# A decoder trunk's causal mask: from a product on TensorE to VectorE's reduction, with the forget gates' sums as rows of a score product

## The chip, the cores and the metric

The kernel runs on one core of a Trainium2 chip. The metric is the device time of one execution in microseconds (us), as the median of several runs. The engines are TensorE (PE: matmuls; PEld: its weight loads), VectorE (DVE), ScalarE (ACT), GpSimd (POOL) and SyncE (SP), whose queue issues nearly all transfers. Each engine works through its own queue in order and waits on semaphores of the others.

## What is computed

A trunk of two layers over 1024 tokens of width 1024. Layer 0 mixes tokens by differential attention (8 heads, each with two score maps), layer 1 by forgetting attention (16 heads, with a gate whose logarithm is summed along the tokens). After each comes a gated MLP with a short convolution. Cut to what matters here:

```python
# layer 0, per block of 128 queries
s = jnp.einsum('bhcqd,bhckd->bhcqk', qb, k) * scale
p = masked_softmax(s, causal_mask(start, Q_BLOCK, S))
a = p[:, :, 0] - lam * p[:, :, 1]
# layer 1
c = jnp.cumsum(jax.nn.log_sigmoid(f_logit + b_f), axis=1)
s = (jnp.einsum('bhqd,bhkd->bhqk', qb, k) * scale
     + cb[..., :, None] - c[..., None, :])
p = masked_softmax(s, causal_mask(start, Q_BLOCK, S))
```

## The kernel before

All big products run as several products of rounded fp32 (fp32r) halves: a value is split into a high part, made by ScalarE (L87), and the rest, made by VectorE (L89), and a product of two split values is three matmuls (`mm3`, L98 to L100). For the scores the halves are stacked: a head has 64 rows, so one matmul over 128 rows holds high times high and low times high (L496), and a second one holds high times low (L497), with a zeroed copy `qz` of the queries that GpSimd fills (L489).

The attention of a layer runs over 8 pairs of heads. For each pair there are 16 score jobs (8 query tiles of 128 for each of two heads or maps). A job of query tile qt covers (qt + 1) x 128 keys in chunks of 512. Between the jobs `attention` steps through the projection of the next pair (48 steps of three 512-wide matmuls), or, for the last pair, through the first half of the output projection (64 steps). These matmuls fill TensorE while VectorE and ScalarE do the softmax; `tick` and `tock` run the later parts of earlier jobs (normalisation, transposes by L1320, value products by L1345 and L98 on `pt`). So the order of the code sets the work, and a scheduler then sets each engine's order.

In a job TensorE first makes the scores in one of two PSUM banks `s`, and then adds the causal mask onto the last 128 columns by one more product: the identity in bf16 (`idb`) as weights and the mask (`mneg` in layer 0, `mpos` in layer 1, whose scores are negated) as the moving operand (L498). In layer 0 VectorE then takes the negated maximum (L517) and ScalarE the exponential with its sum (L520). In layer 1 VectorE adds, in one instruction with the minimum, the gates' sum of each key (L642). For that the sums, which are along one row, are broadcast to all partitions by a transfer (`load_ck`, L621, into the pool `lg`); `cq` holds the queries' sums (L645).

The sums are made at the start of layer 1: `forget_gates` makes the running sums within blocks of 128, and `forget_sums` adds the sums of the blocks ahead by a product with `tri` (L610), stores them to DRAM (L613) and transposes them for `cq` (L615). `first_pair` projects the first pair of heads, with nothing else to fill TensorE. In layer 0 the normalisation after the values uses a product with ones (L549) over squares made by ScalarE (L545).

Of the kernel before, what the change touches and what calls it, by code (L numbers as in the profile page):

```python
# [9 lines left out]
F32 = mybir.dt.float32  # L10
# [44 lines left out]
class Trunk:  # L55
# [64 lines left out]
    def consts(self):  # L120
# [147 lines left out]
    def split_q(self, par, src, scale, sl, lo):  # L268
# [6 lines left out]
    def split_k(self, par, src, sl):  # L275

        a, b = par[0][:, sl], par[1][:, sl]
        self.split(a, par[2][:, sl], src)
        self.move((b[64:], a[64:]), (b[:64], a[64:]), (a[64:], a[:64]))

# [42 lines left out]
    def first_pair_rotary(self, t):  # L323
# [10 lines left out]
        for c in range(2):  # L334
# [7 lines left out]
            for s in range(2):  # L342
                self.result(0, s, c, ps[s], dst[s], t)
# [4 lines left out]
        for c in range(2):  # L348
# [3 lines left out]
            self.result(0, 2, c, ps, dst[2], t)  # L352
# [4 lines left out]
            self.after(2 + 2 * c, self.turn_v, 0, c, dst[2], *t[5:], True)  # L357
        self.ahead(4)

    def first_pair(self, l, t):  # L360
# [4 lines left out]
        for c in range(2):  # L365
            if c == 1:
                self.transposes(self.acc, 1, range(2))
                self.turn_v(l, 0, dst, *t[5:])
# [3 lines left out]
            for s in range(3):  # L372
# [4 lines left out]
                self.result(l, s, c, ps, dst if s == 2 else None, t)  # L377
            if c:
                self.forget_sums()
                self.after(3, self.turn_v, l, c, dst, *t[5:], True)  # L380

    def project(self, l, p, t):
# [5 lines left out]
        for n, (s, c) in enumerate(order):  # L388
# [15 lines left out]
            self.after(D_EV, self.result, l, s, c, ps, dst[s], t)  # L404
# [5 lines left out]
            if s == 2:  # L410
                self.after(D_V[c], self.turn_v, l, c, dst[2], *t[5:], True)
# [3 lines left out]
    def result(self, l, s, c, ps, dst, t):  # L415

        sl = slice(c * 512, c * 512 + 512)
        if dst is not None:
            self.nc.scalar.activation(dst[:, sl], ps, AF.Copy, scale=DH ** -0.5 if s == 0 else 1.0)
        elif s == 0:  # L420
            if c == 0:
                self.qlo = self.tp.tile([P, 1024], F32R, tag="t", name=self.nm("ql"))
            self.split_q(t[:2], ps, -DH ** -0.5, sl, self.qlo[:, sl])
        else:
            self.split_k(t[2:5], ps, sl)

    def halves(self, dst, t, c, j):

        sl = slice(c * 512, c * 512 + 512)
        if j == 0:  # L430
            self.split_q(t[:2], dst[0][:, sl], None, sl, dst[0][:, sl].bitcast(F32R))
        else:
            self.split_k(t[2:5], dst[1][:, sl], sl)
# [1099 lines left out]
```

## Time and profile before

| | us |
|---|---|
| median of 3 runs | 2475.31 (2471.26 to 2476.17) |
| the profiled execution | 2474.66 |
| its span, first to last instruction | 2472.8 |
| attention of layer 0, about | 45 to 530 |
| MLP of layer 0, about | 530 to 1200 |
| attention of layer 1, about | 1214 to 1770 |
| MLP of layer 1, about | 1770 to 2472 |

The mean granted clock of TensorE is 0.998 of full. Durations of matmuls overlap: a matmul's row gives its start and the time until its modelled end, and the next may start long before it. What a matmul costs in a stream is therefore read from start to start. An arrow at a row's end names what ended the idle time ahead of the instruction. The page's other engines are averages over the span; whether they matter is read from who waits for whom.

### The profile page before, as it was taken

What the parts mean: (1) busy time and instruction counts of PE and PEld (TensorE: products, weight loads), DVE (VectorE), ACT (ScalarE), POOL (GpSimd) and SP (SyncE); (2) the same over time, 40 slices, a digit from 0 to 9 for tenths busy, and PEclk for the clock granted to TensorE, in tenths of its full rate; (3) what the DMA queues carried; (4) which work ended last, traced back from release to release, by engine and by line L of the source; (5) the groups of instructions that cost most, each with busy time, mean ns of one, the idle gap of its engine ahead of it and who ended that gap; (6) DMA issues with size and microseconds to landing.
All of it is one profiled execution on the core that took longest, in us unless ns stands there. A gap on an engine that the chain in (4) does not pass through costs nothing. (4 is left out here: it accounts for less than half of the span.)

```text
span 2472.8 us, 33965 instructions
## 1 busy us (share of the span) xinstructions
PE 2436.3 (99%) x12059; PEld 2016.7 (82%) x12059; DVE 1908.3 (77%) x3604; ACT 1256.4 (51%) x2387; POOL 136.3 (6%) x316
## 2 busy tenths in 40 slices
PE   8999999999999999999999999999999999999998
PEld 6888888788888888888778888888888888888886
DVE  5777777989866677887767777778898666668977
ACT  4555655646544444544545555555465444445444
POOL 2001000110000000000101000000010000000000
PEclk9999999999999999999999999999999999999999
DMA  5222222622222223974322222225222222238851
GB/s 174 71 86 79 76 81 84 216 72 99 77 102 78 77 77 131 343 238 154 107 87 78 78 77 76 78 85 172 86 86 102 86 77 77 92 99 315 273 170 68
DMA packets 116793, 289.50 MB, mean 117 GB/s; under 512 B 18032, under 2 KB 25072, under 8 KB 116624
## 3 DMA queue, kind: packets, MB, share of 16 engines
q1 hardware_dynamic: 115824, 285.44, 34.8%
q8 instruction: 95, 1.56, 0.3%
q0 software_dynamic: 800, 1.90, 0.2%
q14 instruction: 74, 0.61, 0.1%
HBM read 196.70 MB, written 59.11 MB: 103 GB/s over the span
## 5 line engine op out<-in xcount | busy, mean ns | idle before, releaser
L98 PE MATMUL m<-xh,wh 128*128 128x512 f32 x768 | 323.1, 421 | 11.2 <-ACT xh L87 10.9
L100 PE MATMUL m<-xh,wl 128*128 128x512 f32 x768 | 303.7, 395 | 0.0
L99 PE MATMUL m<-xl,wh 128*128 128x512 f32 x768 | 301.1, 392 | 0.0
L98 PE MATMUL m<-xh,wo 128*128 128x512 f32 x656 | 255.5, 389 | 0.5 <-ACT pt L1042 0.5
L100 PE MATMUL m<-xh,wo 128*128 128x512 f32 x656 | 255.5, 389 | 0.0
L99 PE MATMUL m<-xl,wo 128*128 128x512 f32 x656 | 255.2, 389 | 0.0
L87 ACT ACTIVATE wo<-wg 128x512 fp32r<-128x512 f32 x168 | 106.2, 632 | 222.4 <-PE m L100 215.8
L87 ACT ACTIVATE pt<-m 128x512 fp32r<-128x512 f32 (+1 forms) x240 | 128.5, 553 | 151.3 <-PE m L1320 112.7
L98 PE MATMUL m<-q,wo 128*128 128x512 f32 x472 | 184.3, 390 | 0.0
L99 PE MATMUL m<-q,wo 128*128 128x512 f32 x472 | 183.8, 389 | 0.0
L100 PE MATMUL m<-q,wo 128*128 128x512 f32 x472 | 183.7, 389 | 0.0
L98 PEld LDWEIGHTS m<-xh,wh 128*128 128x128 f32 x768 | 145.8, 190 | 34.4 <-ACT xh L87 10.9
L100 PEld LDWEIGHTS m<-xh,wl 128*128 128x128 f32 x768 | 144.8, 189 | 32.2 <-DVE wl L89 0.4
L89 DVE TENSOR_TENSOR pt<-m,pt 128x512 fp32r<-128x512 f32 (+1 forms) x240 | 148.5, 633 | 22.2 <-ACT pt L87 19.6
L99 PEld LDWEIGHTS m<-xl,wh 128*128 128x128 f32 x768 | 145.9, 190 | 23.1
L87 ACT ACTIVATE wo<-t 128x512 fp32r<-128x512 f32 x132 | 82.7, 627 | 145.3 <-PE m L100 133.3
L89 DVE TENSOR_TENSOR wo<-wg,wo 128x512 fp32r<-128x512 f32 x168 | 115.4, 688 | 38.5 <-ACT wo L87 37.7
L98 PEld LDWEIGHTS m<-xh,wo 128*128 128x128 f32 x656 | 123.1, 188 | 26.7 <-ACT pt L1042 1.3
L100 PEld LDWEIGHTS m<-xh,wo 128*128 128x128 f32 x656 | 123.1, 188 | 26.3 <-DVE wo L89 0.8
L99 PEld LDWEIGHTS m<-xl,wo 128*128 128x128 f32 x656 | 123.1, 188 | 25.6
L489 POOL CAST qz<-q 64x128 fp32r<-64x128 f32 x256 | 94.4, 370 | 888.4 <-PE s L498 793.2
L496 PE MATMUL s<-q,q 128*128 128x512 f32 (+3 forms) x384 | 130.3, 339 | 0.8 <-ACT p L650 0.8
(333 smaller groups left out, 6165.4 us busy)
## 6 DMA issues: line engine op xcount, KB each, us to landing
wst<-in_w SPq DMA_DIRECT2D x46, 512.0 KB, 3.4
t<-in_wi SPq DMA_DIRECT2D x44, 512.0 KB, 4.3
ha<-ad SPq DMA_DIRECT2D x88, 256.0 KB, 6.2
wg<-in_wi SPq DMA_DIRECT2D x42, 512.0 KB, 3.2
ad<-t SPq DMA_DIRECT2D x42, 512.0 KB, 3.5
q<-q SPq DMA_DIRECT2D x128, 128.0 KB, 2.3
pt<-in_wd SPq DMA_DIRECT2D x24, 512.0 KB, 5.3
hb<-in_wd SPq DMA_DIRECT2D x44, 256.0 KB, 4.5
```

Source lines behind the costliest of these rows:

```text
L87: nc.scalar.activation(hi, src, AF.Copy, scale=1.0 if scale is None else scale)
L89: nc.vector.tensor_tensor(lo, src, hi.bitcast(F32), op=ALU.subtract)
L98: mm(out, wh, xh, start=start, stop=False)
L99: mm(out, wh, xl, start=False, stop=False)
L100: mm(out, wl, xh, start=False, stop=stop)
L489: nc.gpsimd.tensor_copy(qz[r:r + 64, :], q[r:r + 64, qt * P:qt * P + P])
L496: nc.tensor.matmul(sb[:, ks], q[:, qt * P:qt * P + P], kd[:, ks], start=True, stop=False)
```

## The change

The mask's product goes, with its weights and the bf16 identity. A row `mask` of 1024 columns is made instead: zeros, and the negated mask in the last 128 columns. VectorE adds its last (qt + 1) x 128 columns to the scores in the instruction that takes their minimum, in both layers; the scores of layer 0 are negated now as well (by the scale on the queries), and their exponential has a scale of -1. In layer 1 the sums of the keys are no longer broadcast. They are split into a high and a low part, stored to DRAM, and read back as rows 64 and 65 beside the 64 low rows of the keys, which for the second head lie in a tile of their own (`kb`, filled by a transfer). The second score product runs over these 66 rows, with ones in rows 64 and 65 of `qz`, so that both heads use rows 0 to 65. The gates' weights `wf` lie in a working buffer of the pool `prob` in place of one of their own.

```diff
-        self.idb = cp.tile([P, P], BF16, name="idb")
-        nc.vector.tensor_copy(self.idb, self.ident)
-        self.mneg = cp.tile([P, P], BF16, name="mneg")
-        nc.vector.tensor_copy(self.mneg, mask)
-        self.mpos = cp.tile([P, P], BF16, name="mpos")
-        nc.vector.tensor_scalar(self.mpos, mask, -1.0, None, op0=ALU.mult)
+        self.mask = cp.tile([P, S], BF16, name="mask")
+        nc.gpsimd.memset(self.mask[:, :S - P], 0.0)
+        nc.vector.tensor_scalar(self.mask[:, S - P:], mask, -1.0, None, op0=ALU.mult)
...
-        self.move((b[64:], a[64:]), (b[:64], lo[64:]), (a[64:], lo[:64]))
...
+        hi = slice(0, 64) if l else slice(64, P)
+        lo_ = slice(64, P) if l else slice(0, 64)
+        self.move((b[hi], a[64:]), (b[lo_], lo[64:]), (a[64:], lo[:64]))
...
+    def split_k(self, l, p, t, src, sl):
...
+        a, b, lo = t[2][:, sl], t[3][:, sl], t[4][:, sl]
+        self.split(a, lo, src)
         self.move((b[64:], a[64:]), (b[:64], a[64:]), (a[64:], a[:64]))
+        if l:
+            self.move((t[7][:64, sl], lo[64:]))
+            if p:
+                self.sum_rows(p, t, sl)
+
+    def sum_rows(self, p, t, sl):
...
+        for h in range(2):
+            self.nc.sync.dma_start(t[4 + 3 * h][64:66, sl].bitcast(F32), self.cd[:, 2 * p + h, sl])
...
-    def scores(self, q, kd, kl, r, qt, mask):
+    def scores(self, l, q, kd, kl, h, qt):
...
+        r, rows = (0, slice(0, 66)) if l else (64 * h, slice(0, P))
...
             nc.tensor.matmul(sb[:, ks], q[:, qt * P:qt * P + P], kd[:, ks], start=True, stop=False)
-            nc.tensor.matmul(sb[:, ks], qz, kl[:, ks], start=False, stop=not last)
-        nc.tensor.matmul(sb[:, ln - P:ln], self.idb, mask, start=False, stop=True)
-        return sb, ln
+            nc.tensor.matmul(sb[:, ks], qz[rows], kl[rows, ks], start=False, stop=True)
+        mn = self.small(tag="nm")
+        nc.vector.tensor_tensor_reduce(sb[:, :ln], sb[:, :ln], self.mask[:, S - ln:], 1.0, BIG,
+                                       ALU.add, ALU.min, mn)
+        return sb, ln, mn
...
-        nc.vector.tensor_reduce(nmx, sb[:, :ln], axis=AX.X, op=ALU.max, negate=True)
...
-        nc.scalar.activation(pt[:, :ln], sb[:, :ln], AF.Exp, bias=nmx, accum_out=lsum)
+        nc.scalar.activation(pt[:, :ln], sb[:, :ln], AF.Exp, bias=mn, scale=-1.0, accum_out=lsum)
...
-            self.wf = [self.cp.tile([P, 128], F32R, name=f"wf{j}") for j in range(2)]
+            w = self.tmp(F32R, pool=self.pp, tag="p")
+            self.wf = w[:, :P], w[:, P:2 * P]
+            for t in self.qz[0] + self.qz[1]:
+                nc.gpsimd.memset(t[64:66, :].bitcast(F32), 1.0)
...
-        nc.sync.dma_start(self.cd.rearrange("h (b t) -> (h b) t", t=P), c)
+        hl = self.chl[:, :P], self.chl[:, P:]
+        self.split(*hl, c)
+        self.cd = self.dr.tile([2, 16, 1024], F32, name="cd")
+        for j in range(2):
+            nc.sync.dma_start(self.cd[j].rearrange("h (b t) -> (h b) t", t=P), hl[j].bitcast(F32))
+        self.sum_rows(0, t, slice(0, 1024))
...
-        if qt == 0 and (p, h) not in self.ck:
-            self.load_ck(p, h)
-        ck = self.ck[p, h]
-        sb, ln = self.scores(t[h], t[2 + h], t[4], 64 * h, qt, self.mpos)
-        nc.vector.tensor_tensor_reduce(sb[:, :ln], sb[:, :ln], ck[:, :ln], 1.0, BIG,
-                                       ALU.add, ALU.min, mn)
+        sb, ln, mn = self.scores(1, t[h], t[2 + h], t[4 + 3 * h], h, qt)
```

TensorE's queue in layer 0, at a score job in the middle of a pair (L498 is the mask; L549 the product with ones of the normalisation; `pt` are transposed probabilities), before:

```order
L496 MATMUL s_1553<-q_567,q_565 128x512
L549 MATMUL m_1397<-sq_1412,ones 128x256
L497 MATMUL s_1553<-q_568,qz_303 128x512
L496 MATMUL s_1553<-q_567,q_565 128x256
L497 MATMUL s_1553<-q_568,qz_303 128x256
L498 LDWEIGHTS idb
L498 MATMUL s_1553<-mneg,idb 128x128
L98 MATMUL m_1562<-pt_1512,q_569 128x256
```

and of the change:

```order
L507 MATMUL s_1523<-q_565,qz_300 128x512
L560 MATMUL m_1370<-sq_1385,ones 128x256
L506 MATMUL s_1523<-q_564,q_562 128x256
L507 MATMUL s_1523<-q_565,qz_300 128x256
L98 MATMUL m_1531<-pt_1482,q_566 128x256
```

The two entries of the mask are gone, and the product with ones stands behind the first two score products instead of between them; this second move is there in six of the pairs.

VectorE's queue in layer 0 around the reductions over the scores, before (L523 inverts a sum of exponentials, L89 is a split):

```order
L517 TENSOR_REDUCE nm_1948<-s_1944 128x1
L558 SCALAR_TENSOR_TENSOR of_1404<-sq_1873,of_1404 128x256
L89 TENSOR_TENSOR wl_2112<-wst_2009,wh_2111 128x1024
L517 TENSOR_REDUCE nm_1983<-s_1979 128x1
L89 TENSOR_TENSOR pt_1992<-m_1965,pt_1992 128x384
```

and of the change, in the same stage:

```order
L509 ISA s_1842,nm_1845<-s_1842,mask 128x256
L509 ISA nm_1845 128x1
L89 TENSOR_TENSOR pt_1883<-m_1856,pt_1883 128x512
L509 ISA s_1870,nm_1873<-s_1870,mask 128x256
L509 ISA nm_1873 128x1
L534 RECIPROCAL rs_1920<-ls_1847 128x1
```

One instruction becomes two: the addition with its minimum, and the read of the accumulator; what stands behind the read doesn't use its result.

TensorE's queue at the first scores of layer 1, from the product with `tri` on (L496 and L497 of the first query tile), before:

```order
L610 MATMUL m_11942<-p_11830,tri 128x1
L496 MATMUL s_11997<-q_11611,q_11609 128x128
L497 MATMUL s_11997<-q_11613,qz_300 128x128
L615 MATMUL m_11947<-ident,p_11830 128x128
L98 MATMUL m_11960<-xh_11391,wh_11912 128x512
```

of the change, the same place:

```order
L626 MATMUL m_11817<-p_11704,tri 128x1
L506 MATMUL s_11876<-q_11483,q_11481 128x128
L506 MATMUL s_11898<-q_11483,q_11481 128x256
L635 MATMUL m_11827<-ident,p_11704 128x128
L98 MATMUL m_11841<-xh_11260,wh_11787 128x512
```

and where the second products of these two tiles now stand, 37 products of 512 columns further on:

```order
L98 MATMUL m_11887<-xh_11646,wh_11787 128x512
L507 MATMUL s_11876<-q_11485,qz_297 128x128
L507 MATMUL s_11898<-q_11485,qz_298 128x256
L99 MATMUL m_11887<-xl_11647,wh_11787 128x512
L100 MATMUL m_11887<-xh_11646,wl_11788 128x512
```

The first products of two tiles stand together, and their second products, which need the sums' rows, have moved behind the filling work.

## Rows read from the trace of the kernel before

**Rows 1.** The page's part 1: engine, busy us (share), instructions.
```profile
PE 2436.3 (99%) x12059; PEld 2016.7 (82%) x12059; DVE 1908.3 (77%) x3604; ACT 1256.4 (51%) x2387; POOL 136.3 (6%) x316
```

**Rows 2.** Instructions of L498: engine, operation, count, duration ns min/median/max, first and last start.
```profile
L498 PE MATMUL s<-mneg,idb x128: 229/229/233, 49.2 to 514.7; 128*128 128x128 bf16 x128
L498 PE MATMUL s<-mpos,idb x128: 229/230/330, 1268.7 to 1766.5; 128*128 128x128 bf16 x128
```

**Rows 3.** TensorE's timeline, layer 0: start us, duration, engine, line, out<-in, shape.
```profile
307.15 0.23 PE L498 MATMUL s<-mneg,idb 128*128 128x128 bf16 x1
307.19 0.36 PE L98 MATMUL m<-pt,q 128*128 128x256 f32 x1
307.39 0.28 PE L99 MATMUL m<-pt,q 128*128 128x256 f32 x1
307.51 0.28 PE L100 MATMUL m<-pt,q 128*128 128x256 f32 x1
```

**Rows 4.** TensorE's timeline, layer 1, with and without a mask.
```profile
1405.21 0.38 PE L1320 MATMUL m<-ident,t 128*128 128x128 f32 x2
...
1405.66 0.40 PE L99 MATMUL m<-xl,wh 128*128 128x512 f32 x1
...
1407.95 0.22 PE L496 MATMUL s<-q,q 128*128 128x128 f32 x1
...
1408.12 0.23 PE L498 MATMUL s<-mpos,idb 128*128 128x128 bf16 x1
1408.16 0.48 PE L98 MATMUL m<-xh,wh 128*128 128x512 f32 x1
1408.48 0.39 PE L99 MATMUL m<-xl,wh 128*128 128x512 f32 x1
1408.71 0.40 PE L100 MATMUL m<-xh,wl 128*128 128x512 f32 x1
```

**Rows 5.** VectorE's groups by shape: line, operation, out<-in, count, busy us, mean ns.
```profile
L642 DVE CUSTOM_DVE_ANT_0 s<-s,ck 128x1024 f32<-128x1024 f32 x16 | 19.7, 1230 | 6.9 <-PE s L498 6.9
L517 DVE TENSOR_REDUCE nm<-s 128x1 f32<-128x1024 f32 x16 | 19.5, 1218 | 0.4 <-PE s L498 0.4
L642 DVE DVE_READ_ACCUMULATOR2_ANT nm<- 128x1 f32 x128 | 18.1, 141 | 0.0
```

**Rows 6.** VectorE's timeline around a reduction (layer 0) and the two-operand one (layer 1).
```profile
379.02 1.22 DVE L517 TENSOR_REDUCE nm<-s 128x1 f32<-128x1024 f32 x1
380.16 0.41 DVE L453 TENSOR_TENSOR t<-t,rope 128x256 f32<-128x256 f32 x1
1273.16 0.30 DVE L642 CUSTOM_DVE_ANT_0 s<-s,ck 128x128 f32<-128x128 f32 x1
1273.38 0.14 DVE L642 DVE_READ_ACCUMULATOR2_ANT nm<- 128x1 f32 x1
1273.38 0.35 DVE L654 TENSOR_SCALAR p<-p,rs 128x256 f32<-128x256 f32 x1
```

**Rows 7.** Timeline rows at waits, with idle time and its releaser in brackets.
```profile
306.14 0.70 PE L549 MATMUL m<-sq,ones 128*128 128x256 f32 x2 [0.33 <-ACT sq L545]
387.52 0.66 PE L465 MATMUL m<-ident,t 128*128 128x128 f32 x4 [0.98 <-DVE pt L89]
459.92 0.50 PE L98 MATMUL m<-wh,xh 128*128 128x512 f32 x1 [1.80 <-DVE pt L89]
1262.54 0.33 SPq L613 DMA_DIRECT2D cd<-p  x1
1264.82 1.53 SPq L621 DMA_DIRECT2D ck<-cd  x2
1270.67 0.30 DVE L642 CUSTOM_DVE_ANT_0 s<-s,ck 128x128 f32<-128x128 f32 x1 [3.49 <-DMA ck<-cd]
1272.24 0.33 PE L496 MATMUL s<-q,q 128*128 128x128 f32 x1 [0.81 <-ACT p L650]
```

**Rows 8.** Busy us (instructions) of PE, PEld, DVE, ACT, POOL in the fullest stretch; clock, DMA.
```profile
500.00:505.00 5.00, 5.00 (x27) 4.10 (x26) 5.00 (x9) 1.23 (x4) 0.00 (x0) 1.00 0.00 0
```

More of the change, by code (lines that the diff above doesn't have):

```diff
@@ L356, in first_pair_rotary @@
                 self.halves(dst, t, 1, 1)
-            self.after(2 + 2 * c, self.turn_v, 0, c, dst[2], *t[5:], True)
+            self.after(2 + 2 * c, self.turn_v, 0, c, dst[2], *t[5:7], True)
         self.ahead(4)
@@ L376, in first_pair @@
                 self.dense(ps, *self.w[s], c)
-                self.result(l, s, c, ps, dst if s == 2 else None, t)
+                self.result(l, 0, s, c, ps, dst if s == 2 else None, t)
             if c:
-                self.forget_sums()
-                self.after(3, self.turn_v, l, c, dst, *t[5:], True)
+                self.forget_sums(t)
+                self.after(3, self.turn_v, l, c, dst, *t[5:7], True)
     def project(self, l, p, t):
@@ L403, in project @@
                 dst[s] = self.tmp()
-            self.after(D_EV, self.result, l, s, c, ps, dst[s], t)
+            self.after(D_EV, self.result, l, p, s, c, ps, dst[s], t)
             if l == 0 and s == 1:
@@ L410, in project, with result @@
             if s == 2:
-                self.after(D_V[c], self.turn_v, l, c, dst[2], *t[5:], True)
+                self.after(D_V[c], self.turn_v, l, c, dst[2], *t[5:7], True)
             if c:
                 del self.w[i + s]
-    def result(self, l, s, c, ps, dst, t):
+    def result(self, l, p, s, c, ps, dst, t):
         sl = slice(c * 512, c * 512 + 512)
         if dst is not None:
-            self.nc.scalar.activation(dst[:, sl], ps, AF.Copy, scale=DH ** -0.5 if s == 0 else 1.0)
+            self.nc.scalar.activation(dst[:, sl], ps, AF.Copy, scale=-DH ** -0.5 if s == 0 else 1.0)
         elif s == 0:
@@ L514, in diff_scores @@
         nc = self.nc
-        sb, ln = self.scores(t[j], t[2 + j], t[4], 64 * j, qt, self.mneg)
-        nmx, lsum = self.small(tag="nm"), self.small(tag="ls")
-        nc.vector.tensor_reduce(nmx, sb[:, :ln], axis=AX.X, op=ALU.max, negate=True)
+        sb, ln, mn = self.scores(0, t[j], t[2 + j], t[4], j, qt)
+        lsum = self.small(tag="ls")
         yield
         pt = self.tmp(pool=self.wp, tag="wst", bufs=2) if j else self.tmp(pool=self.pp, tag="p")
-        nc.scalar.activation(pt[:, :ln], sb[:, :ln], AF.Exp, bias=nmx, accum_out=lsum)
+        nc.scalar.activation(pt[:, :ln], sb[:, :ln], AF.Exp, bias=mn, scale=-1.0, accum_out=lsum)
         yield
@@ L604, in forget_gates, with forget_sums @@
         self.c = c
-    def forget_sums(self):
+    def forget_sums(self, t):
         nc, c = self.nc, self.c
@@ L635, in fox_scores @@
         cq = self.cq[:, 2 * p + h, qt:qt + 1]
[L636 to L643 removed]
+        sb, ln, mn = self.scores(1, t[h], t[2 + h], t[4 + 3 * h], h, qt)
+        lsum = self.small(tag="ls")
         nc.vector.scalar_tensor_tensor(mn, mn, cq, cq, op0=ALU.subtract, op1=ALU.add)
[L646 to L647 removed]
         yield
@@ L670, in attention @@
         self.od = self.dr.tile([NP, P, 1024], F32, name=f"od{l}")
-        tiles = lambda p: [self.qtile((p + l) % 2) for _ in range(7)]
+        tiles = lambda p: [self.qtile((p + l) % 2) for _ in range(7)] + \
+            ([self.lp.tile([P, 1024], F32R, tag="lg", name=self.nm("kb"))] if l else [])
         self.slabs = [self.i[f"w{l}"][s * NP + p] for p in range(NP) for s in range(3)]
@@ L674, in attention @@
         self.w, self.stage, self.queue = {}, {}, []
-        self.ofs, self.ck = {}, {}
+        self.ofs = {}
         if l == 1:
```

33 lines of the change are left out of this document (10 added, 23 removed).

## The prediction

> **What bounds the kernel now.** I read the page's busy times first [rows 1]. TensorE is busy for 2436.3 of 2472.8 us, so only 36.5 us of the span can be anything but its own work; VectorE is busy for 77%. A saving on TensorE's path is therefore worth its full time as long as nothing else becomes late, and a cost on another engine is worth nothing as long as TensorE doesn't wait for it. Next I asked for the line that the change takes out: L498 has 128 matmuls in each layer, each with a weight load of the identity ahead [rows 2]. Then I read TensorE's timeline around a few of them, start to start, because the durations in the page overlap (a 512-wide matmul "takes" 0.39 us while the next starts 0.23 us later) and so say nothing about what one costs. Last come TensorE's waits, and the stretch where VectorE is fullest [rows 7, 8].
>
> **The change, part by part.**
>
> *The mask's product goes.* Behind a 256-wide score product the mask starts at 307.15, the next product (256 wide) at 307.19 and the one after that at 307.39 [rows 3]. Mask and one 256-wide product together take 0.24 us; the next product alone takes 0.12 us (307.39 to 307.51). The mask's price is 0.12 us: 0.04 of its own and 0.08 that shows as a longer step of the product behind it. Where the last score products are only 128 wide, the price is less: L496, L497, mask and one 512-wide product take from 1407.95 to 1408.48, 0.53 us, and two 128-wide transposes with a 512-wide product behind them, without a mask, from 1405.21 to 1405.66, 0.45 us [rows 4]. So 0.08 us there. With 512 columns behind it the mask costs 1408.16 to 1408.48 less the ordinary step 1408.48 to 1408.71, plus its own 0.04: 0.13 us. Two of the eight query tiles (tiles 0 and 4, whose last chunk is 128 wide) take the low price: 64 x 0.08 + 192 x 0.12 = 28.2 us. The bounds are 256 x 0.04 = 10.2 us, if the long step behind stays whatever stands in front of it, and 256 x 0.13 = 33.3 us. I take 28.2, since the two transposes show that a short product costs its 0.11 us each and leaves nothing behind ((0.45 - 0.23) / 2).
>
> The Trainium skill (TensorE: Matmul & The Clock Gate, Back-to-back issue gap) gives a 128-wide matmul at 2.4 GHz about 56 ns in a stream; by that alone the sum would be 14 us instead of 28. The rows disagree with it here: the step from mask to the second product behind is 0.12 us longer, not 0.06.
>
> *VectorE adds the mask, layer 0.* 128 maximum reductions become 128 of the two-operand instruction that layer 1 already uses, each with an accumulator read behind it. By durations this looks dear: 1230 for 1218 ns at 1024 wide, plus 141 ns for the read [rows 5], 0.153 us x 128 = 19.6 us. But the step decides. The two-operand one starts at 1273.16, its read at 1273.38, and the next, independent instruction starts at 1273.38 too [rows 6]: the read costs the engine nothing there. The step of 0.22 us is 0.08 below the duration of 0.30, just as the reduction's step of 1.14 us is 0.08 below its 1.22 (379.02 to 380.16) [rows 6]. What is left is the difference of durations, 0.012 us x 128 = 1.5 us over the 480 us of layer 0's attention, off TensorE's path. The exponential behind it waits for the read and starts some 0.14 us later; it frees a score bank that TensorE nowhere waits for in layer 0. I price this part at nothing, with 19.6 us as its upper end. In layer 1 the same instruction reads a bf16 mask in place of an fp32 row; no row of before shows that operand. Bounds: as now, or slower by the read of the other 128 (0.141 x 128 = 18 us, on an engine that idles for 23%); I take as now.
>
> *The gates' sums as two rows of the second product, layer 1.* The product keeps its columns and contracts 66 rows instead of 128. No matmul of before contracts fewer than 128 rows, so this isn't shown. The nearest rows are the 128-row products at 0.23 us for 512 columns [rows 4]; I take the same, and price the other end below as a rival. The Trainium skill (the same page, LDWEIGHTS) says that a weight load's time goes by its columns and that its row count doesn't matter, which speaks for no change. The sixteen broadcasts of a sum to all partitions (L621) go; per pair of heads and half there are three small transfers more, on SP's queue (one 64-row move, two of two rows). The transfer that overwrites two rows of what the move reads waits for it to land, 2.3 us by the gap between store and load in [rows 7], and behind it in SP's queue stand the next weight fetch and moves whose data are products steps away; price nothing, at worst 14 such waits of 2.3 us on a queue that no engine then waits for.
>
> *Layer 1's first scores.* Here the sums are now needed by TensorE itself, not only by VectorE. Now the sums are stored at 1262.54, their loads are issued at 1264.82, and VectorE, which waited 3.49 us for them, goes on at 1270.67 [rows 7]. After the change a split stands ahead of the store (two small instructions, some 0.6 us by VectorE's 0.3 us each [rows 6]), the store takes the same 2.3 us, and the small load between 2.3 us and the old one's 5.9: the rows are there between 1268 and 1271. The order puts the second products behind 37 further 512-wide ones after the sums' product, 37 x 0.23 = 8.5 us, so from about 1262 they stand past 1270. I take 1 us of loss there, 0 to 3 us as bounds; there is a wait of 0.81 us at this place already, for a score bank (1272.24) [rows 7].
>
> *What is late next.* TensorE now waits once per pair in layer 0 for the square that the normalisation takes (0.33 us at 306.14, with half a microsecond lost in all, between two score products); the order puts that product one place later, which gives back about 0.23 us x 6 = 1.3 us. Against it, TensorE arrives earlier at the waits for VectorE's splits: 0.98 us at 387.52 at the end of a pair, 1.80 us at 459.92 where the output projection begins [rows 7]. These chains run over VectorE and a weight fetch and don't become faster. Over the two or three score groups since the last meeting I take 0.25 us for each of 7 pairs = 1.8 us, and 1.3 us for each of the two last pairs, where VectorE is full (5.00 of 5.00 us at 500) [rows 8]: 2.6 us.
>
> *Small parts.* The mask's memset on POOL stands among the first memsets, which POOL has done long before the first scores; the gates' weights move into a working buffer, which is split after the down projection has released it, while ScalarE idles. Nothing.
>
> **Sum.** -28.2 - 1.3 + 1.0 + 1.8 + 2.6 = -24.1 us. The profiled execution took 2474.7 us (span 2472.8); that gives 2450.6, and against the median, 0.65 us higher, 2451 us.
>
> **The rivals.**
> 1. *The step behind remains.* The 0.08 us behind a mask is the price of going from a score group to another kind of product, and the last score product inherits it. Then between the mask's own step, 0.04 us, and the low price of 0.08 us goes everywhere: 10.2 to 20.5 us, 15 in the middle. With the other terms unchanged, 2475.3 - 15 - 1.3 + 5.4 = 2464. For it: the last score product is then what a different product follows. Against it: the transposes in rows 4 leave no such step. The Trainium skill's 56 ns per mask (section above) would end here too.
> 2. *VectorE's reads count in full.* If the reads wait in layer 0, 19.6 us stand on a queue that is full at each pair's end and in the last pair, and TensorE waits for it: 2451 + 19.6 = 2471, within the measurement. Against it: the step in rows 6.
> 3. *Slower: 66 rows cost more.* Layer 1's second products have 16 heads x 36 x 128 = 73,728 columns, at 0.23 us per 512 some 33 us. If a product over a part of the rows ran at half speed, this adds 33 us: 2484, slower than before. It decides from a factor of 1.7 (24 / 33 + 1). Nothing in the profile speaks for it.
> 4. *The change doesn't do what it says:* the order shows the 512 TensorE entries gone, so I leave this at nothing.
>
> **How the numbers follow.** Forecast 0.70 (2443 to 2460), rival 1 0.11, rival 2 0.07, rival 3 0.06; 0.06 for what I don't see. A measurement of this kernel can tell about 0.2%, 5 us, from no change. Faster: 0.70 + 0.11 + 0.04 = 0.85; same 0.07 + 0.01 = 0.08; slower 0.06 + 0.01 = 0.07. The range reaches from 2442 (33.3 saved, with nothing lost but the first scores' 1 us and some of the waits) to 2466, so that rival 1 is in it and no more than 2 in 10 is out.
>
> **What would show it.** In the changed profile: no L498; the product behind a 256- or 512-wide score group steps 0.12 or 0.23 us like its neighbours (rival 1: 0.2 or 0.32). VectorE's instruction behind an accumulator read in layer 0 starts with it (rival 2: 0.14 later, and longer TensorE waits for the splits). The step of a 512-wide second product in layer 1 stays at 0.23 us (rival 3: more). The wait at 459.92 grows by about a microsecond. TensorE's busy time falls by some 25 to 28 us, and its unbusy 36.5 us grow by at most 6. I'm wrong if the waits on VectorE or on the sums' transfers grow by more than 10 us together.

## The result and the profile after

The changed kernel takes 2455.6 us (median of 4 runs, 2455.07 to 2458.51) against 2475.05 for the kernel before (four runs, one more than in the table above): a ratio of 0.9926, interval 0.9909 to 0.9944, so 14 to 23 us less. The profiled execution took 2455.07 us, its span is 2453.3. The prediction was 2451.0 with a range from 2442 to 2466.

The page's part 1 of the changed kernel, to be held against [rows 1]:

```profile
PE 2414.2 (98%) x11803; PEld 2014.8 (82%) x11803; DVE 1911.1 (78%) x3731; ACT 1256.6 (51%) x2388; POOL 137.6 (6%) x321
```

TensorE has 256 products less and is busy 22.1 us less; of 2453.3 us it is not busy in 39.1, before in 36.5. VectorE's busy time hardly moves.

Where the time went, from the first scores of each layer, the first and last score product of each pair, and the first transposes of the MLPs, in the two traces:

| stretch | before, us | after, us | saved | 16 masks a pair at 0.091 |
|---|---|---|---|---|
| to the first score | 48.88 | 47.91 | 1.0 | |
| layer 0, pair 0 | 50.19 | 50.92 | -0.7 | 1.5 |
| layer 0, pairs 1 to 6 | 349.02 | 342.68 | 6.3 | 8.7 |
| layer 0, last pair to the MLP's transposes | 107.81 | 108.16 | -0.4 | 1.5 |
| MLP 0 and first pair's projection | 706.15 | 705.67 | 0.5 | |
| layer 1, pair 0 | 56.82 | 55.35 | 1.5 | 1.5 |
| layer 1, pairs 1 to 6 | 376.32 | 368.45 | 7.9 | 8.7 |
| layer 1, last pair to the MLP's transposes | 112.27 | 108.09 | 4.2 | 1.5 |
| MLP 1 | 665.32 | 666.06 | -0.7 | |

The two layers lose the same 128 masks, yet layer 1 becomes 13.5 us shorter and layer 0 only 5.2.

TensorE's timeline of the changed kernel, at a score group in layer 0 whose last product is 128 columns wide, at one whose last is 256 wide, and at a second score product over 66 rows in layer 1 (start us, duration, engine, line, out<-in, shape, idle time and its releaser):

```profile
269.60 0.27 PE L507 MATMUL s<-q,qz 128*128 128x128 f32 x1
269.71 0.33 PE L98 MATMUL m<-pt,q 128*128 128x256 f32 x1
269.88 0.28 PE L99 MATMUL m<-pt,q 128*128 128x256 f32 x1
...
303.13 0.47 PE L506 MATMUL s<-q,q 128*128 128x256 f32 x1
303.44 0.28 PE L507 MATMUL s<-q,qz 128*128 128x256 f32 x1
303.56 0.28 PE L98 MATMUL m<-pt,q 128*128 128x256 f32 x1
303.67 0.28 PE L99 MATMUL m<-pt,q 128*128 128x256 f32 x1
...
1393.43 0.39 PE L506 MATMUL s<-q,q 128*128 128x512 f32 x1
1393.66 0.40 PE L507 MATMUL s<-kb,qz 66*128 66x512 f32 x1
1393.89 0.28 PE L1354 MATMUL m<-pt,q 128*128 128x256 f32 x1
```

Behind the 256-wide group the next product now steps 0.11 us (303.56 to 303.67) like its neighbours, where behind a mask it stepped 0.20 [rows 3]: no long step remains. Behind the 128-wide group a part of it remains without any mask: 0.17 us (269.71 to 269.88), and 0.171 in the median of 35 such places. The 66-row product steps 0.23 us (1393.66 to 1393.89), as 128 rows do.

VectorE's timeline around a 1024-wide addition of the mask in layer 0:

```profile
380.50 1.22 DVE L509 CUSTOM_DVE_ANT_0 s<-s,mask 128x1024 f32<-128x1024 f32 x1
381.64 0.14 DVE L509 DVE_READ_ACCUMULATOR2_ANT nm<- 128x1 f32 x1
381.64 0.41 DVE L569 SCALAR_TENSOR_TENSOR of<-sq,of 128x256 f32<-128x256 f32 x1
```

From the addition to the next instruction it is 1.14 us, the step that the maximum had [rows 6]; the read of the accumulator starts together with what stands behind it. TensorE's waits in layer 0, with those of [rows 7] in mind:

```profile
94.55 0.39 PE L98 MATMUL m<-pt,q 128*128 128x256 f32 x1 [0.77 <-DVE pt L89]
...
333.53 0.39 PE L98 MATMUL m<-pt,q 128*128 128x256 f32 x1 [1.04 <-DVE pt L89]
360.47 0.70 PE L560 MATMUL m<-sq,ones 128*128 128x256 f32 x2 [0.45 <-ACT sq L556]
446.71 0.55 PE L1329 MATMUL m<-ident,p 128*128 128x128 f32 x3 [1.10 <-DVE p L541]
455.64 0.50 PE L98 MATMUL m<-wh,xh 128*128 128x512 f32 x1 [1.76 <-DVE acc L807]
```

The first stands near the end of the first pair, the second 7 us into a pair, and neither product waited before; the third comes in six pairs (0.33 before); the last two stand in the last pair. The waits that stood at the pairs' ends, such as 0.98 us at 387.52 [rows 7], are gone.

### The profile page after: what moved, and what is told of

The parts are those of the page before. It is cut to its first block, busy times and chain, and to the rows that moved or that the text cites. A ratio compares the mean times of both kernels' runs of the same rounds, so it can differ in the third digit from the quotient of the medians.

```text
span 2453.3 us, 33606 instructions
## 1 busy us (share of the span) xinstructions
PE 2414.2 (98%) x11803; PEld 2014.8 (82%) x11803; DVE 1911.1 (78%) x3731; ACT 1256.6 (51%) x2388; POOL 137.6 (6%) x321
## 5 line engine op out<-in xcount | busy, mean ns | idle before, releaser
L509 DVE CUSTOM_DVE_ANT_0 s<-s,mask 128x128 f32<-128x128 f32 (+7 forms) x256 | 194.3, 759 | 49.2 <-PE s L507 48.6
L89 DVE TENSOR_TENSOR pt<-m,pt 128x512 fp32r<-128x512 f32 (+1 forms) x240 | 148.5, 633 | 20.6 <-ACT pt L87 17.6
L89 DVE TENSOR_TENSOR wo<-wg,wo 128x512 fp32r<-128x512 f32 x168 | 115.4, 688 | 38.8 <-ACT wo L87 37.8
```

The source lines that it names most:

```text
L89: nc.vector.tensor_tensor(lo, src, hi.bitcast(F32), op=ALU.subtract)
L509: nc.vector.tensor_tensor_reduce(sb[:, :ln], sb[:, :ln], self.mask[:, S - ln:], 1.0, BIG, ALU.add, ALU.min, mn)
```

## Experiments

The theory at this point: a mask is worth about 0.09 us wherever TensorE sets the pace; layer 0 gives half of that back, because TensorE now comes early to chains that it doesn't set; layer 1 gains more than its masks. Each ratio below is against the kernel before on the same chip, where its median was 2472.0 to 2473.4 us. One execution of each kernel by stage, in us (each row sums to the span), shows at a glance what follows:

| kernel | to first score | layer 0 | MLP 0 | layer 1 | MLP 1 |
|---|---|---|---|---|---|
| before | 48.9 | 507.0 | 706.2 | 545.4 | 665.3 |
| after | 47.9 | 501.8 | 705.7 | 531.9 | 666.1 |
| e5, after again | 47.6 | 499.8 | 705.7 | 531.6 | 666.1 |
| e1, layer 0 alone | 47.2 | 502.9 | 707.0 | 544.8 | 666.9 |
| e2, layer 1 alone | 47.9 | 507.0 | 707.3 | 530.9 | 668.1 |
| e3, no mask in layer 0 | 47.6 | 501.2 | 707.1 | 548.5 | 667.6 |
| e4, both in layer 0 | 48.5 | 507.2 | 704.9 | 544.6 | 665.9 |
| e6, mask product twice | 47.0 | 519.1 | 706.8 | 549.8 | 667.4 |
| e7, mask product kept in layer 1 | 48.6 | 501.6 | 708.6 | 542.7 | 667.8 |
| e8, product with ones later | 47.3 | 511.6 | 710.1 | 531.5 | 665.7 |
| e9, weight 3 | 47.3 | 508.6 | 705.8 | 530.8 | 666.5 |
| e10, no deduction | 47.5 | 510.1 | 706.9 | 531.3 | 665.5 |
| e11, weight 4 | 47.7 | 507.3 | 706.9 | 531.4 | 666.9 |
| e12, one broadcast less | 47.2 | 504.3 | 707.2 | 543.9 | 665.0 |

Stages with the same code differ between the traces by some us: layer 0 as before takes 504.3 to 507.2 (before, e2, e4, e12), with its masks gone 499.8 to 502.9 (after, e1, e3, e5, e7). So layer 0 gives some 5 of 11.6 us by all nine, and a difference of 2 us between two single traces tells nothing.

### One layer at a time

```diff
 # e1: layer 0 of the kernel before
-        nc.tensor.matmul(sb[:, ln - P:ln], self.idb, mask, start=False, stop=True)
+        if mask is not None:
+            nc.tensor.matmul(sb[:, ln - P:ln], self.idb, mask, start=False, stop=True)
...
-        nc.vector.tensor_reduce(nmx, sb[:, :ln], axis=AX.X, op=ALU.max, negate=True)
+        nc.vector.tensor_tensor_reduce(sb[:, :ln], sb[:, :ln], self.mask[:, S - ln:], 1.0, BIG,
+                                       ALU.add, ALU.min, nmx)
```

> The kernel before with layer 0 alone changed: no mask product there, VectorE adds the mask and takes the minimum, scores negated; layer 1 stays as before. (Two small buffers are placed elsewhere so that it fits: one bf16 mask is dropped and the gates' weights lie in a working buffer.) The trace of the changed kernel gives 0.096 us per mask left out, 128 x 0.096 = 12.3 us in layer 0, of which only about 5 us show in the layer's length. Theory (the masks' time is partly given back inside layer 0, and the two layers are additive): 5 us below the kernel before, 3 to 8. Rival (layer 0's missing 7 us were taken by something that the change in layer 1 brings, such as another order of the whole): 12 us below.

Measured: 2473.3 us, ratio 1.0001 (0.999 to 1.0013). Layer 0 itself became 4.2 us shorter, as the theory has it, and so did the traced execution as a whole (2470.55 against 2474.66 us), but the median shows no gain, and the runs spread from 2466.8 to 2481.7. Among them those with a mean granted clock of 0.999 took 2470.6 us in the mean (5 runs), those with 0.997 2475.8 (3 runs). The clock doesn't explain the missing gain: the kernel before took 2470.9 us at 0.999 on this chip (13 runs). What hides it stays open.

```diff
 # e2: layer 0 of the changed kernel set back
+        if l == 0:
+            nc.tensor.matmul(sb[:, ln - P:ln], self.idb, self.mneg, start=False, stop=True)
+            nc.vector.tensor_reduce(mn, sb[:, :ln], axis=AX.X, op=ALU.max, negate=True)
+            return sb, ln, mn
```

> The changed kernel with layer 0 set back to the kernel before (mask product and VectorE's maximum), so layer 1 alone is changed. Theory, additive layers: 13.5 us below the kernel before (the length of layer 1's attention in the two traces), 11 to 16. Rival (the two layers share the loss by the order that the scheduler makes): about 18 us below, with layer 0 then no shorter by itself.

Measured: 2462.7 us, ratio 0.9956 (0.9942 to 0.997), 7 to 14 us less. Layer 1 is 14.5 us shorter, as expected, and the MLPs are 3.9 us longer (2.4 in e1). Within its layer each change does about the same alone as together with the other; the whole doesn't add up (0 and -10 against -17.5 to -19.5), and the stages say where a part of it is: the two MLPs, whose code is the same but for the place of the gates' weights, take between 1370.7 and 1376.5 us together. VectorE's and ScalarE's instructions stand in the same order in the MLPs of before, after, e2, e5 and e7, and two executions of the changed kernel agree there to 0.01 us. What differs is waits of up to 2 us, such as this one of e7, on VectorE and behind it on TensorE:

```profile
2362.05 0.69 DVE L1174 TENSOR_TENSOR hb<-hb,hb 128x512 f32<-128x512 f32 x1 [1.70 <-DMA hb<-tb]
...
2370.28 0.50 PE L98 MATMUL s<-wo,oa 128*128 128x512 f32 x1 [2.02 <-DVE acc L1241]
```

VectorE waits for a fetched block, and TensorE for VectorE. Why a block lands later in one kernel than in another with the same MLP stays open.

### VectorE or TensorE: what gives layer 0's time back

```diff
 # e3: no mask product in layer 0, VectorE's maximum as before
-        sb, ln = self.scores(t[j], t[2 + j], t[4], 64 * j, qt, self.mneg)
+        sb, ln = self.scores(t[j], t[2 + j], t[4], 64 * j, qt, None)
 # e4: mask product kept, and VectorE adds zeros as it takes the minimum
+        nc.gpsimd.memset(self.mask, 0.0)
...
-        nc.vector.tensor_reduce(nmx, sb[:, :ln], axis=AX.X, op=ALU.max, negate=True)
+        nc.vector.tensor_tensor_reduce(sb[:, :ln], sb[:, :ln], self.mask[:, S - ln:], 1.0, BIG,
+                                       ALU.add, ALU.min, nmx)
```

> The kernel before with layer 0's mask product left out and nothing in its place: VectorE's maximum stays as it was, so layer 0 leaves out the causal mask within the diagonal tiles. It takes TensorE's 128 mask products away at an unchanged VectorE. Theory A (layer 0 gives time back because TensorE arrives earlier at chains that it doesn't pace): about 5 us below the kernel before, like layer 0 with VectorE's mask, 3 to 8. Rival V (it is given back by VectorE's two-operand instruction, its accumulator read, or the later exponential): 12 us below the kernel before.

> The kernel before with layer 0's mask product kept, and VectorE's maximum replaced by the two-operand instruction of the changed kernel, which here adds zeros; scores negated. It is VectorE's part of the change alone, at unchanged TensorE work. Theory A: no change, within 2 us, since the accumulator read costs the engine nothing and VectorE is not what layer 0 waits for. Rival V: 5 to 8 us above the kernel before; if the reads count in full on a full queue, up to 19.6 us above.

Measured: e3 2470.3 us, ratio 0.9991 (0.9981 to 1.0001); e4 2473.7 us, ratio 1.0006 (0.9997 to 1.0014). With the masks out and VectorE untouched, layer 0 still gains only 5.8 us of about 11.6; with VectorE's instruction and all masks it loses 0.2. So the loss doesn't need VectorE's instruction, and rival V falls. VectorE's part costs at most 3.5 us by e4; that it is free isn't shown, since the two comparisons that differ by it and by the place of the gates' weights alone come out longer in the medians, e4 over before by 1.2 us and e1 over e3 by 3.1.

Where the rest went can be seen in part. TensorE's waits of more than 0.15 us in layer 0 sum to 6.7 us before, 10.4 in e3 and 11.2 in the changed kernel. The split that the wait at 333.53 names, and the same split and product before:

```profile
332.79 0.69 DVE L89 TENSOR_TENSOR pt<-m,pt 128x512 fp32r<-128x512 f32 x1 [0.45 <-ACT pt L87]
...
335.81 0.69 DVE L89 TENSOR_TENSOR pt<-m,pt 128x512 fp32r<-128x512 f32 x1 [0.45 <-ACT pt L87]
337.06 0.36 PE L98 MATMUL m<-pt,q 128*128 128x256 f32 x1
```

Counted from the pair's first score (326.39 after, 330.85 before) the split starts at 6.4 us instead of 5.0, while TensorE without the wait would be there at 6.1 instead of 6.2: the pair begins sooner, and VectorE's chain has not kept up. Why is only argued. That TensorE runs ahead of a chain with its own pace is one reading. The other is the order: the scheduler made a new one when the masks went, in which 164 of VectorE's 834 instructions in layer 0 and 111 of TensorE's 2597 stand elsewhere. After, e1, e3, e5 and e7 all have the new order, and before, e2, e4 and e12 the old one; no run takes the masks out in the old order, so this rival stands.

### The chip's own spread, and the price of a mask

e5 is the changed kernel unchanged, run beside the next three.

> The changed kernel once more, on the chip on which the next three run, to have its time beside theirs and a second trace. Theory: 2455.6 us as in its first runs, 17 to 20 us below the kernel before. Its waits of more than 0.6 us stand where they stood: at the starts of layer 0's pairs (94, 333, 391 us), at 446 and 456 us in the last pair, and none at layer 1's first scores (1260 to 1275) and in layer 1's last pair (1690 to 1705). Rival (those two waits come and go from run to run): one of them, 1.4 to 2.6 us, is back.

Measured: 2454.6 us (2452.4 to 2458.0), ratio 0.9931 (0.9919 to 0.9944). The waits stand where they stood, but for one more of 0.96 us at 276.23, and no wait of this size is back at layer 1's first scores or in its last pair. Layer 0's last pair is 2.3 us shorter than in the first trace (105.8 against 108.2): the wait at 454.75 is 1.32 us, not 1.76, and the granted clock stays at 1.00 behind it, where it was 0.57 for 4 us.

```diff
 # e6
-        nc.tensor.matmul(sb[:, ln - P:ln], self.idb, mask, start=False, stop=True)
+        nc.tensor.matmul(sb[:, ln - P:ln], self.idb, mask, start=False, stop=False)
+        nc.tensor.matmul(sb[:, ln - P:ln], self.idb, self.zero, start=False, stop=True)
```

> The kernel before with a second product like the mask's behind each mask, of zeros, with the same weights (the identity) loaded again: 256 products more. Layer 1's pairs last 62.65 us before, with gaps of 0.23 us that don't move, so the pair's length reads the price. If each such product costs the 0.096 us that the removed masks gave back: 16 x 0.096 = 1.5 us a pair, 64.2 us, and 20 to 25 us in the whole. If the price of the prediction holds (0.08 and 0.12 us, 28.2 us in all): 64.4 us. If most of the price is the change from one kind of product to another, so that a second one of the same kind costs its step alone, 0.04 to 0.06 us: 63.3 to 63.6 us a pair and 10 to 15 us in the whole.

Measured: 2490.2 us, ratio 1.0077 (1.0063 to 1.009). Layer 1's pairs take 63.36 us, 0.71 more: 0.044 us for each second product. TensorE's timeline at the end of a pair of layer 0 and at one of these products in layer 1:

```profile
276.29 0.55 PE L467 MATMUL m<-ident,t 128*128 128x128 f32 x3 [1.44 <-DVE sq L560]
...
1423.75 0.28 PE L499 MATMUL s<-q,qz 128*128 128x256 f32 x1
1423.87 0.23 PE L500 MATMUL s<-mpos,idb 128*128 128x128 bf16 x1
1423.93 0.22 PE L501 MATMUL s<-zero,idb 128*128 128x128 bf16 x1
1423.96 0.36 PE L1348 MATMUL m<-pt,q 128*128 128x256 f32 x1
```

So the third case holds in layer 1: a first bf16 product between fp32r ones costs 0.091 us (61.20 to 62.65 us a pair), a second one half of it. About half of a mask's price is thus paid once per group. That this half is the change from one kind of product to another isn't shown: behind a 128-wide product of the same kind a part of the long step is there too (0.17 us at 269.71), so a short product alone may make it. The whole is longer than that case said, 16 to 22 us instead of 10 to 15, and the rest is in layer 0: 12.1 us more, of which 128 x 0.044 = 5.6 are the products; the row at 276.29 is one of the new waits at the pairs' ends. In layer 0 a shift in either direction costs some 6 us beyond the products themselves; here, too, the order in the queues changed with it.

```diff
 # e7
+        if l:
+            nc.tensor.matmul(sb[:, ln - P:ln], self.idb, self.mask[:, :P], start=False, stop=True)
```

> The changed kernel with a mask product put back in layer 1 alone (identity times zeros, same place and size as before; VectorE still adds the mask, the sums stay rows of the second product). It parts layer 1's gain into the mask's product and the sums' way. Theory (of layer 1's 13.5 us some 10 to 12 are the mask products, and the rest is the waits at the first scores and in the last pair, which went with the broadcast of the sums): pairs back at 62.65 us, 11 to 12 us above the changed kernel, that is about 2467, 6 to 8 us below the kernel before; the waits at 1270 and 1700 us stay away. Rival (the waits come from the order around the masks): they come back, and the time is 15 to 17 us above the changed kernel, about 2472.

Measured: 2471.1 us, ratio 0.9996 (0.9988 to 1.0005). In its stage the theory holds: the pairs are back at 62.68 us (0.093 us a mask), layer 1 is 10.8 us longer than in the changed kernel, and the waits stay away. In the whole the rival's number came, 16.6 us, because the MLPs and the start took 5.7 us more than in e5, which neither expected. Layer 1's gain thus parts into 10.8 us for the masks and 2.7 us (545.4 to 542.7) for the sums' way, or 2 us against e1 and e4, whose layer 1 is that of before too (544.8 and 544.6).

### Why layer 1 gained more than its masks

Transfers (SPq: start and duration of the issue), ScalarE and TensorE in layer 1's last pair before the change, then the clock there (us, busy us of PE, PEld, DVE, ACT, POOL with instructions, granted clock, DMA share, GB/s):

```profile
1690.92 0.32 SPq L621 DMA_DIRECT2D ck<-cd  x1
1691.29 0.90 SPq L792 DMA_DIRECT2D acc<-hd  x2
1693.66 0.32 SPq L773 DMA_DIRECT2D t<-od  x1
...
1701.65 0.63 ACT L87 ACTIVATE xh<-t 128x512 fp32r<-128x512 f32 x1 [1.90 <-DMA t<-od]
...
1703.53 0.73 PE L98 MATMUL m<-wh,xh 128*128 128x512 f32 x1 [1.96 <-DVE pt L89]
```

```profile
1704.00:1708.00 4.00, 4.00 (x19) 3.12 (x18) 2.70 (x7) 1.27 (x3) 0.00 (x0) 0.62 0.00 0
```

and the same place in e7, whose sums are rows:

```profile
1690.66 0.32 SPq L787 DMA_DIRECT2D t<-od  x1
1691.08 0.38 SPq L1414 DMA_DIRECT2D lg<-in_ln_g  x1
...
1694.88 0.62 ACT L87 ACTIVATE xh<-t 128x512 fp32r<-128x512 f32 x1
```

Before, the last broadcast of a sum (512 KB) is issued at 1690.92 with two more blocks of 512 KB right behind it; the fetch issued at 1693.66 is awaited until 1701.65, TensorE stands for 1.96 us, and then its granted clock is 0.62 for 4 us: most of that stretch at the lower of its two levels, 1.2 GHz in place of 2.4. In e7 the broadcast isn't there, and the fetch issued at 1690.66 is used at 1694.88. The last run takes that one transfer away:

```diff
 # e12
     def load_ck(self, p, h):
+        if (p, h) == (NP - 1, 1):
+            self.ck[p, h] = self.ck[p, 0]
+            return
```

> The kernel before without the last of its sixteen broadcasts of a sum (that of layer 1's last head, one transfer of 512 KB issued at 1690.92 us); the head takes the row of its neighbour instead, so this head's gate is left out of the computation. Nothing else is changed, and VectorE's instructions stay. Theory (the 1.96 us at which TensorE stands in layer 1's last pair, at 1703.5, and the fall of its clock behind it, come from the transfers: the broadcast waits in SP's queue for its buffer and holds two fetches of 512 KB, which then crowd the fetch that ScalarE waits for): that wait goes, layer 1's last pair up to the MLP's first transposes takes about 109 us instead of 112.3, and the whole 2 to 3.5 us less than the kernel before, 2469 to 2470. Rival (the wait belongs to VectorE's work or the order there): 112 us and no change in the whole.

Measured: 2469.9 us, ratio 0.9988 (0.9979 to 0.9996). The whole is as the theory has it; the stage is half so. ScalarE's use of this fetch and of the next one, and TensorE's longest wait there, from the timeline:

```profile
1694.88 0.63 ACT L87 ACTIVATE xh<-t 128x512 fp32r<-128x512 f32 x1 [0.17 <-DMA t<-od]
...
1700.53 0.63 ACT L87 ACTIVATE xh<-t 128x512 fp32r<-128x512 f32 x1 [1.88 <-DMA t<-od]
...
1702.86 0.33 PE L1323 MATMUL m<-ident,p 128*128 128x128 f32 x1 [1.43 <-DVE acc L801]
```

The fetch arrives in time, 4.5 us after its issue, and the wait for it is gone. But the next fetch, issued at 1694.33, comes 6.2 us after its issue; ScalarE waits 1.88 us for it and TensorE, behind VectorE's accumulation, 1.43, and the last pair takes 110.6 us, not 109. Other kernels take as long with the broadcast in place. The same place in e1, and the clock behind:

```profile
1697.28 0.63 ACT L87 ACTIVATE xh<-t 128x512 fp32r<-128x512 f32 x1 [1.37 <-DMA t<-od]
...
1699.17 0.50 PE L98 MATMUL m<-wh,xh 128*128 128x512 f32 x1 [1.43 <-DVE pt L89]
```

```profile
1700.00:1704.00 4.00, 3.79 (x27) 3.17 (x26) 3.84 (x10) 2.57 (x7) 0.29 (x1) 1.00 0.28 58
```

The last pair takes 110.5 us in e1 and 110.6 in e4, where TensorE waits 1.43 and 1.60 us and the clock stays at 1.00; before, with the lower clock, it takes 112.3. So the broadcast makes this fetch late (7.4 to 8.0 us from issue to landing in the five traces with it, 4.5 in e12) and with it the wait at 1703.5. The 1.7 us that the stage gained in e12 are no more than what the fall of the clock cost before (4 us at 0.62 lose 1.5), and that fall doesn't come in every execution. With the sums as rows and the masks kept, e7, the pair takes 109.3 us: 1.2 less than e1 and e4. Why the second fetch is late in e12 was not tested.

The first scores of layer 1 show the same thing more loosely. In e3, whose layer 1 is that of before (timeline, then the stretch behind):

```profile
1266.33 0.30 DVE L643 CUSTOM_DVE_ANT_0 s<-s,ck 128x128 f32<-128x128 f32 x1 [5.33 <-DMA ck<-cd]
...
1267.90 0.34 PE L496 MATMUL s<-q,q 128*128 128x128 f32 x1 [2.65 <-ACT p L651]
```

```profile
1268.00:1272.00 4.00, 4.00 (x16) 3.43 (x17) 2.38 (x14) 1.81 (x7) 0.58 (x2) 0.57 0.29 66
```

VectorE, which waited 3.49 us for the broadcast in the trace of before [rows 7], waits 5.33 here, TensorE stands for 2.65 us instead of 0.81, and its clock falls. With broadcasts, layer 1's first pair takes from 56.8 to 58.0 us, and 60.2 in e3, where the clock falls; with the sums as rows 56.5 with the mask products (e7) and 55.34 to 55.39 without them in seven executions.

### Can layer 0's loss be had back?

```diff
 # e8
-FL = 1
+FL = 2
 # e9 (e11 with 4 in place of 3; in e10 W_V is 0 in place of 1)
-            total, acc, base = sum(j[0] + 1 + W_C for j in jobs) - (W_V * 10 if l == 0 else 0), 0, done
+            total, acc, base = sum(j[0] + 1 + (W_C if l else 3) for j in jobs) - (W_V * 10 if l == 0 else 0), 0, done
```

> The changed kernel with layer 0's product with ones issued one step of the pipeline later (the constant FL from 1 to 2). In the changed kernel TensorE waits 0.45 us for ScalarE's square at that product once in each of six pairs, and stands still for 0.62 us there. Theory (these waits are part of what layer 0 gives back): they go, 6 x 0.62 = 3.7 us below the changed kernel, 2 to 4. Rival (the time only moves to the next wait of the pair, for VectorE's splits, since the pair's length isn't set by TensorE): the pairs keep their 57 us and the time stays within 1 us of the changed kernel.

> The changed kernel with layer 0's filling work spread a little differently: each score job's constant weight W_C is 3 instead of 2 there, so one step of three 512-wide products more stands ahead of the value products at a pair's start, where TensorE waits 0.3 to 1.0 us for VectorE's split of the transposed probabilities, and correspondingly fewer stand at the long tiles. Theory (layer 0 gives the masks' time back because TensorE now reaches VectorE's splits early): the waits at the pairs' starts (161, 219, 276, 333, 391 us) go, 2 to 4 us below the changed kernel, if VectorE's later queue lets it; 2451 to 2453. Rival (VectorE's and the transfers' chain sets a pair's length, so filling moves the wait to the pair's end): no gain, 2455 to 2460, with a new wait of 1 to 2 us at the transposes at a pair's end.

> The changed kernel with layer 0's filling work given to each score job without a deduction for the value products that come due (W_V from 1 to 0): at a pair's start two steps stand ahead of the transposes and two ahead of the value products, where there was one each. Theory: as with the weight of 3, the waits at the pairs' starts go, 2 to 4 us below the changed kernel. Rival: the wait moves to the pair's end or to the middle of the pair, and the time stays at 2455 or goes up by as much as the 12 us of the kernel whose product with ones came later.

> As the kernel with the weight of 3, with W_C of 4 in layer 0: still less filling at the long tiles. Theory: no further gain over the weight of 3, since the pair's start has its step already, within 2 us of it. Rival: the long tiles at the pair's end now have too little filling for VectorE's long instructions, and the pairs get longer by 1 us each, 6 us above the weight of 3.

Measured: e8 2466.8 us, ratio 0.9976 (0.9966 to 0.9985); e9 2463.4, 0.996 (0.9948 to 0.9972); e10 2465.9, 0.9972 (0.9962 to 0.9982); e11 2461.9, 0.9956 (0.9943 to 0.9969). All are slower than the changed kernel (e5: 0.9919 to 0.9944; only the interval of e11 touches this). e8 removed the 0.45 us in most pairs and got six waits of 1.9 to 2.7 us; in e9 and e11 the wait left the starts of the later pairs and came up at their ends, larger. TensorE's timeline in e8 with the stretch around it, in e9 and in e11:

```profile
157.14 1.12 PE L475 MATMUL m<-ident,t 128*128 128x128 f32 x4 [2.65 <-DVE pt L89]
```

```profile
156.00:160.00 4.00, 2.86 (x9) 2.48 (x10) 3.67 (x7) 3.44 (x8) 0.00 (x0) 0.63 0.18 41
```

```profile
155.04 0.66 PE L475 MATMUL m<-ident,t 128*128 128x128 f32 x4 [1.96 <-DVE sq L568]
```

```profile
152.14 0.33 PE L1329 MATMUL m<-ident,p 128*128 128x128 f32 x1 [1.16 <-DVE pt L89]
155.61 0.66 PE L475 MATMUL m<-ident,t 128*128 128x128 f32 x4 [1.29 <-DVE pt L89]
```

The rival's mechanism holds, and for e8 and e9 its price was too small: the 342.7 us of pairs 1 to 6 became 350 to 355 each time. In e10 the time came as its rival had it. The one expectation of the theory that held is that e11 lies within 2 us of e9. No version beats the changed kernel.

## Why the prediction was right, and where it was not

The mechanism and the sign were right: TensorE was the bound, the masks lay on its path, and 17.5 to 19.5 us of an expected 24 came. That the sum came so near is in part luck: it hides wrong terms that partly cancel.

- **The mask's product, -28.2 us: mis-sized.** The pairs of layer 1 give 0.091 us a mask, e7 0.093: 256 x 0.091 = 23.3 us. Read step by step, from the last score product to the second product behind it, a mask costs 0.10 us in the mean of the 235 groups that have the same widths there in both traces and no wait, 25.5 us in all; in layer 1, too, some 0.2 us of a pair are given back. The 0.08 behind a 128-wide score product and the 0.12 behind a wider one were right (0.075 and 0.12) where a product of 256 or 512 columns follows. The step that failed is that the price had been taken by the group alone: where 128-wide transposes follow (49 masks) it is 0.07, and 0.05 if the group's last product is 128 wide as well. The lower bound of 10.2, rival 1, fell with the step at 303.56. Its mechanism holds in part behind 128-wide products (the step at 269.71), which is why a mask costs less there; the 0.13 of the upper bound was read at such a place, where a part of the long step stays without a mask. The Trainium skill (TensorE: Matmul & The Clock Gate, Back-to-back issue gap) gives, beside the 56 ns that the prediction quoted and that leave out the weight load, 81 ns for a 128-wide matmul with its weight load in a sustained stream. The measured 91 are near to that, and the second product's 44 are below both.
- **VectorE's addition, 0 us: right within the measurement** (e4, at most 3.5 us; the step at 380.50). Rival 2 fell.
- **66 rows, no change: right** (0.23 us at 1393.66). Rival 3 fell. The Trainium skill (same page, LDWEIGHTS) says that the rows of a weight load don't count. The trace agrees: loads over 66 rows take 188 to 189 ns in the median, over 128 rows 188.
- **The product with ones one place later, -1.3 us: wrong sign.** The wait grew from 0.33 to 0.45 us in six pairs, +0.7 us. The product moved by one score product, but TensorE came earlier by more than that.
- **TensorE earlier at VectorE's splits in layer 0, +1.8 and +1.3 us: the sign right, the size too small.** By the table 2.2 us were given back in pair 0, 2.4 in pairs 1 to 6 (with the product with ones) and 1.8 in the last pair: 6.4 in place of 1.8 (3.1 less the 1.3), and 4.4 with e5's trace. The failed step is 0.25 us a pair: it looked only at the waits that were there, which went, and the new ones stand elsewhere, most of them some 7 us into a pair. Whether TensorE's early arrival makes them or the new order stays open.
- **Layer 1's first scores, +1.0 us: nothing was lost.** The loads were issued at 1261.73 and the second products ran at 1264.94 without a wait, and the old wait of 0.81 us went with the broadcast. That the order had moved these products behind filling work was read rightly.
- **Layer 1's last pair, +1.3 us: wrong sign, -2.7.** The step that failed is the broadcasts that go, which stood without a price. They were not on any engine's queue but SP's, and the last of them held two fetches and crowded a third. Some 1.5 of the 2.7 us are the lower clock behind the wait in the one trace of before.
- **The signs.** TensorE's busy time fell by 22.1 us, not by 25 to 28, and its unbusy time grew by 2.6, within the 6. The wait at 459.92 didn't grow: its place in the last pair has 1.76 us (455.64).

Together, in the two traces: -23.3 + 6.4 + 0.8 (layer 1's pairs 1 to 6) - 2.7 - 0.7 (start and MLPs) = -19.5 us, the difference of the two spans.

## What to carry to other kernels

A product taken off the engine that sets the pace is worth its full step only where that engine also sets the pace of the chain around it; read the waits by stage, and expect new ones at the places where a chain over other engines was just in time. Where a scheduler sets the order, compare the orders of two kernels before giving a cause: a product that is taken out can change both the work and the order. Price a short product by what follows it, and price a large transfer that goes by the fetches that stand behind it in its queue. Before a gain in one trace is called a cause's, look at the same stage in every trace that kept the cause. Parts that are measured alone need not add up: here some of the differences went into waits in stages that neither part touches.

## What the runs showed of the hardware

- A bf16 product of 128 columns between fp32r products costs 0.05 to 0.12 us by the widths around it, 0.091 in the lengths of layer 1's pairs; a second one behind it 0.044 (e6). Behind a 128-wide fp32r product a 256-wide one steps 0.17 us instead of 0.12.
- The read of the accumulator behind a two-operand reduction costs VectorE nothing when the next instruction doesn't need it (1.14 us from addition to next instruction with it, 1.14 for a plain reduction without).
- TensorE's granted clock fell to the lower level for most of a stretch of 4 us at or behind 11 of the 26 waits of 1.76 us or longer that the traces show between the first scores and the last 30 us (0.57 in 456 to 460 of the changed kernel behind the wait of 1.76, 0.62 behind the 1.96 at 1703.53). It stayed at 1.00 behind the other 15, of 1.79 to 2.53 us, as in e1 behind 1.97 us at 1268.41. Four us at 0.57 do the work of 2.3, so such a wait can cost about twice its length. e8, with six waits of 1.9 to 2.7 us, ran from 2461.9 to 2469.9 us: its runs with a mean clock of 0.999 took 2461.9 us (2 runs), those with 0.996 2468.8 (3 runs). That the clock alone parts them was not tested.

```profile
456.00:460.00 4.00, 4.00 (x15) 3.33 (x14) 2.77 (x10) 1.71 (x5) 0.27 (x1) 0.57 1.00 341
```
